# Writing a feed-forward turn's words back over the product tile

## The chip, the cores and the metric

One core of a Trainium2 chip runs the whole kernel. The metric is the device time of one execution in microseconds (us). Every time below is from runs of the kernel before, or from one profiled execution of it. Engines: PE is TensorE (PEld its weight loads), DVE is VectorE, ACT is ScalarE, POOL is GpSimd, SP issues most of the DMAs.

## The reference

A two-layer encoder over 256 tokens of width 2048. A layer is a token mixer with a memory attention, and then a dense SwiGLU feed-forward block, which is the part that matters here:

```python
D_FF = ((8 * D_MODEL // 3 + 255) // 256) * 256   # 5632
def swiglu(h, w_gate_up, w_down):
    gate, up = jnp.split(h @ w_gate_up, 2, axis=-1)
    return (jax.nn.silu(gate) * up) @ w_down
...
x = x + jnp.concatenate([tok_out, mem_out], axis=-1) @ w_out[l]
x = x + swiglu(rms_norm(x, g_ffn[l]), w_gate_up[l], w_down[l])
```

All of it is float32.

## The kernel before

**Products in three parts.** A float32 operand is split into a high part (a cast to fp32r on ACT) and a low part (the operand less the high part, on DVE). A product is three matmuls: high by high (L199), low of the activations by high of the weights (L200), high of the activations by low of the weights (L201). Weights come by DMA into `raw` tiles (4 of them), and `halves` (L263) makes `whi` on ACT (L269) and `wlo` on DVE (L270), in **three** tiles of each name. Activations are split by `split` (L189: high part L193, low part L194) into tiles with the tag `a`.

**The feed-forward block.** The 5632 hidden columns are 11 blocks of 512 (`f`), worked in three chunks of 4, 4 and 3 blocks (L778). For each block a `Pair` (L325) computes gate and up over all 2048 input features; a step `i` takes 256 of them. Then ACT applies Silu into a product tile `sg` (L804), DVE multiplies by the up part in place (L805), and the product is turned, so that hidden columns lie on partitions, and split (L782 to L794). `sg` has two tiles, one for each half `t` of the tokens. When the blocks of a chunk are through, two down `Pair`s multiply the chunk's turned products by the rows of `w_down`, and add into the residual `X`, columns 0 to 1023 in the first pair and 1024 to 2047 in the second.

**Slow and fast steps.** A slow step (`eight`) is 24 matmuls from one weight tile: for t = 0 those into the banks 2 and 3, and then for t = 1 those into 4 and 8. A fast step (`seven`) uses seven products instead of eight (21 matmuls); it needs sums of the weights (`T`, made on DVE at L362 to L365, with a cast and a low part of its own) and sums of the activations (`activation_sums`, two `a` tiles). In a down pair of the first two chunks the fast steps are the first and the third of eight. Four banks go to the tag `acc` and four to `m`; at the end of a pair DVE adds the four `acc` banks to `X` (L428).

**The turn.** `turned` (L207) turns a tile without PE: it takes two `a` tiles, copies the tile's 16-bit halves as two planes into the first (L212), starts a transposing DMA into the second (L213), and some ticks later copies the halves back together into the first (`finish`, L216). That first tile, now the turned words, is what `split_a` reads, once or twice on ACT and once on DVE.

**The `a` tiles of the block.** The pool has 26. At the end of one of the first two chunks are alive: 6 (sums of the input for three fast steps, used by all gate/up pairs), 4 (sums for the two fast down steps, used by both down pairs), and 16 (high and low parts of four blocks and two halves). The planes' tile of the last turn is alive besides until its split has read it.

**What sets the order.** The program's author defers pieces of work by a count of ticks (`later`, `tick`). After that a scheduler puts each engine's instructions into an order of its own, and gives an instruction a tile when one comes free. At run time each engine works through its instructions strictly in that order, and waits at each for what it needs.

Of the kernel before, what the change touches and what calls it, by code (L numbers as in the profile page):

```python
# [12 lines left out]
U16 = mybir.dt.uint16  # L13
# [41 lines left out]
def encoder(ctx: ExitStack, tc: tile.TileContext, x, mem, g_mix, g_ffn, w_in_a, g_v_a, w_spatial, b_spatial,  # L55
            w_in_b, g_q_b, g_k_b, g_mem, w_mem_kv, g_mq, g_mk, w_out, w_gate_up, w_down, rope_c, rope_s, out):
    nc = tc.nc
# [14 lines left out]
    def nm(s):  # L72
        uid[0] += 1
        return f"{s}_{uid[0]}"

    def big(dt=F32, shape=None):
        return room["p"].tile(shape or [P, NB], dt, tag="a", name=nm("a"))
# [19 lines left out]
    def later(delay, fn):  # L97
        queue.append((clock[0] + delay, len(queue), fn))
# [39 lines left out]
    def gslice(kind, l):  # L138
        return gcol[kind][:, 16 * l:16 * l + 16]
# [49 lines left out]
    def split(src, shape):  # L189

        hi = big(F32R, shape)
        lo = big(F32R, shape)
        nc.scalar.copy(hi, src)  # L193
        nc.vector.tensor_tensor(lo, src, hi.bitcast(F32), ALU.subtract)  # L194
        return hi, lo
# [8 lines left out]
        for c in range(4):  # L204
            nc.tensor.transpose(dst[:, c * P:(c + 1) * P], src[:, c * P:(c + 1) * P], ident)  # L205

    def turned(src, ticks, then):  # L207


        a, b = big(F32, [P, 4, P]), big(F32, [P, 4, P])  # L210
        planes, back = [i.bitcast(U16).rearrange("p c n -> p (c n)") for i in (a, b)]
        nc.scalar.copy(planes.rearrange("p (h n) -> p h n", h=2), src.bitcast(U16).rearrange("p (n h) -> p h n", h=2))  # L212
        nc.scalar.dma_start_transpose(back.rearrange("p (c n) -> p c n", n=P), planes)  # L213

        def finish():
            nc.scalar.copy(planes.rearrange("p (n h) -> p n h", h=2), back.rearrange("p (h n) -> p n h", h=2))  # L216
            then(a)

        later(ticks, finish)

# [94 lines left out]
    def activation_sums(a0, a1):  # L315

        q = big(F32, [P, 4, P])
        nc.vector.tensor_tensor(q[:, 0], a1[:, 0], a1[:, 1], ALU.subtract)
        nc.vector.tensor_tensor(q[:, 2], a1[:, 0], a0[:, 0], ALU.subtract)
        nc.vector.tensor_tensor(q[:, 1], a0[:, 0], q[:, 0], ALU.subtract)  # L320
        nc.vector.tensor_tensor(q[:, 3], a0[:, 1], q[:, 1], ALU.subtract)
        hi, lo = split(q, [P, 4, P])
        return [(hi[:, i, :], lo[:, i, :]) for i in range(4)]
# [277 lines left out]
    def add_residual(acc, j, norm, g, parts, dma):  # L601

        def turn(t):
            if dma:
                turned(X[t][j], 2, lambda a: gained(a.rearrange("p c n -> p (c n)"), t, j, g, parts, kept))
            else:
                norm_piece(X[t][j], t, j, g, parts, kept)
            norm.add(X[t][j], t, j)
            if j == 3 and t == NT - 1:
                norm.finish()  # L610

        for t in range(NT):
            if acc:
                nc.vector.tensor_tensor(X[t][j], acc[t], X[t][j], ALU.add)
            later(1 + t, lambda t=t: turn(t))

    def residual_turns(j, norm, g, parts):
        add_residual(None, j, norm, g, parts, j < 2)
# [4 lines left out]
    for l in range(DEPTH):  # L623
# [105 lines left out]
        else:  # L729
# [12 lines left out]
            for c in range(3):  # L742
                acc = linear(hT, w, c * NB)
                attend(head_norm(acc, norm.r, ghead["q"], True), (5, 6, 10, 13), lambda: own["k"], lambda: own["v"],
                       lambda h, c=c: (4 * c + h) // 3, 4 * c, cat)
# [32 lines left out]
        for chunk in (range(0, 4), range(4, 8), range(8, 11)):  # L778
            aT, aS, half = Parts(), {}, {}
            quick = [2 * f + 1 for f in chunk[:2 if chunk[-1] < 10 else l]]  # L780

            def turn_a(a, t, f, aT=aT, aS=aS, half=half, quick=quick):  # L782
                turned(a, 2, lambda whole: split_a(whole, t, f, aT, aS, half, quick))

            def split_a(whole, t, f, aT, aS, half, quick):
                i = 2 * f + 1
                if i in quick:
                    half[i, t] = big(F32, [P, 2, P])
                    nc.scalar.copy(half[i, t], whole[:, 2:4])
                    if t == NT - 1:  # L790
                        aS[i] = activation_sums(half[i, 0], half[i, 1])
                hi, lo = split(whole, [P, 4, P])
                for i in range(4):
                    aT.put(4 * f + i, t, hi[:, i, :], lo[:, i, :])  # L794

            pairs = {}
            for f in chunk:
                order, some = ((3, 4, 5, 0, 6, 1, 7, 2), 2) if f == 0 else ((0, 3, 1, 4, 2, 5, 6, 7), 3)
                pairs[f] = Pair(hF, sums, w_gate_up[l], f * NB, DFF + f * NB, order, fast[:some])
            for f, g in pairs.items():  # L800
                g.run(pairs.get(f + 1))
                for t in range(NT):
                    a = kp.tile([P, NB], F32, tag="sg", name=nm("sg"), bufs=2)
                    nc.scalar.activation(a, g.out[t][0], AF.Silu, scale=norm.r[t])  # L804
                    nc.vector.scalar_tensor_tensor(a, g.out[t][1], norm.r[t], a, ALU.mult, ALU.mult)  # L805
                    later(3 + t if f == chunk[-1] else 12 + t, lambda a=a, t=t, f=f: turn_a(a, t, f))
            last = chunk[-1] == 10
            every = [2 * f + c for f in chunk for c in range(2)]
            slow = [i for i in every if i not in quick]
            pairs = []  # L810
            for jj in range(2):
                order = list(slow)
                for n, i in enumerate(quick):
                    order.insert(2 * n + (2 if last else 0), i)
                into = [[X[t][2 * jj + n] for n in range(2)] for t in range(NT)]
                pairs.append(Pair(aT, aS, w_down[l], 2 * jj * NB, (2 * jj + 1) * NB, order, quick, into))
            for jj, g in enumerate(pairs):
                g.run(None if jj else pairs[1])
                for j in (2 * jj, 2 * jj + 1):
                    if last and l < DEPTH - 1:  # L820
                        residual_turns(j, next_norm, gslice("mix", l + 1), hT)
                    elif last:
                        for t in range(NT):
                            parts = 2 if j == 3 and t == NT - 1 else 1
                            for i in range(parts):
                                cs = slice(i * NB // parts, (i + 1) * NB // parts)
                                eng = nc.scalar if i else nc.sync
                                eng.dma_start(out[0, t * P:(t + 1) * P, j * NB + cs.start:j * NB + cs.stop],
                                              X[t][j][:, cs])
# [37 lines left out]
```

## Time and profile before

| | us |
|---|---|
| median of three runs | 2030.12 |
| lowest and highest of them | 2028.54, 2031.21 |
| the profiled execution | 2030.63 |
| its span, first to last instruction | 2028.8 |
| its mean granted clock of TensorE | 0.998 |

How the views below are read. A row of the timeline is the start in us from the span's start, the duration in us, engine, line, operation, the tile written `<-` the tiles read, and in brackets the idle time of the engine before it with what ended it. A row of a list of waits is who waited for whom, the total in us, the number of waits, and the longest. A row of windows is the stretch, its length, then for PE, PEld, DVE, ACT and POOL the busy time with the number of instructions, then the granted clock of TensorE (1.00 is full speed), the DMA share, and GB/s. Tile names stand without their numbers. The recorded durations of consecutive instructions of one engine overlap a little, so the pace is read from starts.

### The profile page before, as it was taken

How to read it: one execution, taken by the hardware profiler on the slowest of the kernel's cores; microseconds unless marked ns; L12 is line 12 of the kernel's file. 1: busy time of each engine (PE TensorE's matmuls, PEld its weight loads, DVE VectorE, ACT ScalarE, POOL GpSimd, SP SyncE). 2: the span in 40 equal slices, each digit the busy share in tenths (PEclk: the TensorE clock that was granted, in tenths of full speed). 3: DMA queues.
4: the chain of work that ended last, by engine and by line, in shares of the span. 5: the costliest groups of instructions: out<-in, count | busy, mean ns of one | idle time of the engine just before them, and what ended most of it. 6: DMA issues, size and time to landing. Idle time of an engine off the chain costs nothing.

```text
span 2028.8 us, 24312 instructions
## 1 busy us (share of the span) xinstructions
PE 2006.1 (99%) x9058; PEld 1656.6 (82%) x9058; DVE 1603.5 (79%) x1862; ACT 1213.8 (60%) x1509; POOL 50.5 (2%) x80
## 2 busy tenths in 40 slices
PE   8999999999999999999999999999999999999999
PEld 7888888888788887888888888888887888878887
DVE  5576558998889988798666886599987899878977
ACT  7765476666445664456756765756654467634662
POOL 2010000000000000000010100000000000000000
PEclk9999999999999999999999999999999999999999
DMA  9754575666656666577766444756765566755564
GB/s 331 246 183 150 184 218 170 233 198 209 212 184 234 191 214 206 188 231 220 227 203 207 157 144 145 218 187 206 239 218 187 186 203 219 226 188 202 193 212 145
DMA packets 265791, 411.79 MB, mean 203 GB/s; under 512 B 74428, under 2 KB 74792, under 8 KB 265672
## 3 DMA queue, kind: packets, MB, share of 16 engines
q1 hardware_dynamic: 198800, 385.79, 56.3%
q10 hardware_dynamic: 64824, 18.02, 4.8%
q0 software_dynamic: 2048, 6.42, 1.0%
q8 instruction: 71, 1.16, 0.2%
q14 instruction: 48, 0.39, 0.1%
HBM read 390.26 MB, written 4.19 MB: 194 GB/s over the span
## 4 chain that ended last, share of the span: by engine, by line
PE 92%; DVE 3%; DMA 3%; ACT 1%; issue 1%; SPq 0%; DVEq 0%; ACTq 0%
PE acc L201 26%; PE acc L200 26%; PE acc L199 26%; PE m L201 4%; PE m L199 4%; PE m L200 4%; DMA a<-a 2%; DVE wlo L270 2%; ACT whi L269 1%; PE m L205 1%; PE m L515 0%; DMA x<-in_x 0%; PE m L661 0%; DVE T L365 0%; DMA raw<-in_w_in_a 0%
## 5 line engine op out<-in xcount | busy, mean ns | idle before, releaser
L270 DVE TENSOR_TENSOR wlo<-raw,whi 128x2048 fp32r<-128x2048 f32 (+2 forms) x465 | 839.0, 1826 | 242.8 <-ACT whi L269 235.8
L269 ACT CAST whi<-raw 128x2048 fp32r<-128x2048 f32 (+2 forms) x465 | 702.1, 1537 | 459.7 <-PE acc L200 376.5
L199 PE MATMUL acc<-whi,h 128*128 128x512 f32 x1440 | 562.6, 391 | 0.4 <-ACT whi L269 0.4
L200 PE MATMUL acc<-whi,h 128*128 128x512 f32 x1440 | 561.9, 390 | 0.0
L201 PE MATMUL acc<-wlo,h 128*128 128x512 f32 x1440 | 518.2, 391 | 0.8 <-DVE wlo L270 0.8
L199 PE MATMUL acc<-whi,a 128*128 128x512 f32 x1062 | 413.8, 392 | 2.5 <-DVE x L428 1.4
L200 PE MATMUL acc<-whi,a 128*128 128x512 f32 x1062 | 415.6, 391 | 0.0
L201 PE MATMUL acc<-wlo,a 128*128 128x512 f32 x1062 | 400.6, 391 | 0.8 <-DVE wlo L270 0.8
L201 PEld LDWEIGHTS acc<-wlo,h 128*128 128x128 f32 x1440 | 270.6, 188 | 56.9 <-DVE wlo L270 1.4
L199 PEld LDWEIGHTS acc<-whi,h 128*128 128x128 f32 x1440 | 270.6, 188 | 55.5 <-ACT whi L269 0.8
L200 PEld LDWEIGHTS acc<-whi,h 128*128 128x128 f32 x1440 | 270.6, 188 | 55.4
L199 PEld LDWEIGHTS acc<-whi,a 128*128 128x128 f32 x1062 | 199.7, 188 | 46.5 <-DVE x L428 3.0
L201 PEld LDWEIGHTS acc<-wlo,a 128*128 128x128 f32 x1062 | 200.2, 188 | 43.9 <-DVE wlo L270 2.7
L200 PEld LDWEIGHTS acc<-whi,a 128*128 128x128 f32 x1062 | 200.3, 189 | 41.3 <-DVE a L194 0.6
L269 ACT CAST whi<-T 128x1536 fp32r<-128x1536 f32 x82 | 121.4, 1481 | 132.9 <-PE acc L200 99.1
L270 DVE TENSOR_TENSOR wlo<-T,whi 128x1536 fp32r<-128x1536 f32 x82 | 143.9, 1755 | 20.7 <-ACT whi L269 20.7
L199 PE MATMUL m<-whi,a 128*128 128x512 f32 x264 | 103.5, 392 | 5.7 <-ACT whi L269 5.7
L200 PE MATMUL m<-whi,a 128*128 128x512 f32 x264 | 102.8, 390 | 0.0
L216 ACT COPY a<-a 128x1024 uint16<-128x1024 uint16 x60 | 70.2, 1170 | 37.3 <-DMA a<-a 37.1
L201 PE MATMUL m<-wlo,a 128*128 128x512 f32 x264 | 88.7, 395 | 2.4 <-DVE wlo L270 2.4
L362 DVE TENSOR_TENSOR raw<-raw 128x512 f32<-128x512 f32 x82 | 56.5, 688 | 22.8 <-DMA raw<-in_w_gate_up 22.8
L199 PEld LDWEIGHTS m<-whi,a 128*128 128x128 f32 x264 | 49.6, 188 | 18.4 <-ACT whi L269 8.3
(131 smaller groups left out, 1520.0 us busy)
## 6 DMA issues: line engine op xcount, KB each, us to landing
raw<-in_w_gate_up SPq DMA_DIRECT2D x352, 512.0 KB, 4.4
raw<-in_w_down SPq DMA_DIRECT2D x176, 512.0 KB, 5.1
raw<-in_w_out SPq DMA_DIRECT2D x32, 1024.0 KB, 5.2
raw<-in_w_in_a SPq DMA_DIRECT2D x24, 1024.0 KB, 5.1
raw<-in_w_in_b SPq DMA_DIRECT2D x24, 1024.0 KB, 5.0
raw<-in_w_mem_kv SPq DMA_DIRECT2D x16, 1024.0 KB, 5.0
raw<-in_w_in_a SPq DMA_DIRECT2D x7, 512.0 KB, 6.1
x<-in_x SPq DMA_DIRECT2D x8, 256.0 KB, 5.7
```

The lines of the kernel that those rows point to most:

```text
L199: nc.tensor.matmul(out, lhsT=a[0], rhs=b[0], start=start, stop=False)
L200: nc.tensor.matmul(out, lhsT=a[1], rhs=b[0], start=False, stop=False)
L201: nc.tensor.matmul(out, lhsT=a[0], rhs=b[1], start=False, stop=stop)
L205: nc.tensor.transpose(dst[:, c * P:(c + 1) * P], src[:, c * P:(c + 1) * P], ident)
L216: nc.scalar.copy(planes.rearrange("p (n h) -> p n h", h=2), back.rearrange("p (h n) -> p n h", h=2))
L269: nc.scalar.copy(hi[:, cut], raw[:, cut])
L270: nc.vector.tensor_tensor(lo[:, cut], raw[:, cut], hi[:, cut].bitcast(F32), ALU.subtract)
L362: nc.vector.tensor_tensor(raw[:, 0], raw[:, 0], raw[:, 1], ALU.add)
```

## The change

`turned` gets a switch `over`, which only the feed-forward turn sets. With it the second step writes the words back over the tile that they came from, the `sg` tile, and not over the planes' `a` tile; `split_a` then reads the `sg` tile. The turns of the residual are as before.

```diff
-    def turned(src, ticks, then):
+    def turned(src, ticks, then, over=False):
...
         def finish():
-            nc.scalar.copy(planes.rearrange("p (n h) -> p n h", h=2), back.rearrange("p (h n) -> p n h", h=2))
-            then(a)
+            words = src.rearrange("p (c n) -> p c n", c=4) if over else a
+            halves = (src.bitcast(U16) if over else planes).rearrange("p (n h) -> p n h", h=2)
+            nc.scalar.copy(halves, back.rearrange("p (h n) -> p n h", h=2))
+            then(words)
...
             def turn_a(a, t, f, aT=aT, aS=aS, half=half, quick=quick):
-                turned(a, 2, lambda whole: split_a(whole, t, f, aT, aS, half, quick))
+                turned(a, 2, lambda whole: split_a(whole, t, f, aT, aS, half, quick), True)
```

Behind L216 the lines of the changed kernel have numbers that are 2 higher (L270 becomes L272, L428 becomes L430). Every engine has as many instructions as before. On ACT, POOL and SP their order is the same too; on DVE and PE it differs in four stretches, the down pairs of the first and second chunk of each layer. The first of the four:

On PE, at the handover of the first down pair (banks `acc_691`, `acc_692`, `acc_693`, `acc_700`) to the second (`m_737` to `m_740`, `acc_741` and on), in the kernel before. The first number of a name is the tile's. Weights 726 and 730 are the first pair's last two steps, 733 and 735 the second pair's first, fast step (735 is from its T); `a_710` and `a_711` are the high and low part of the chunk's last block for t = 1, `a_561` and `a_562` sums for the fast step:

```order
L201 MATMUL acc_742_4415<-wlo_734_4388,a_561_3418 128x512
L199 MATMUL m_739_4403<-whi_735_4391,a_561_3418 128x512
L200 MATMUL m_739_4403<-whi_735_4391,a_562_3419 128x512
L199 MATMUL m_740_4407<-whi_735_4391,a_561_3418 128x512
L200 MATMUL m_740_4407<-whi_735_4391,a_562_3419 128x512
L201 MATMUL m_739_4403<-wlo_736_4392,a_561_3418 128x512
L201 MATMUL m_740_4407<-wlo_736_4392,a_561_3418 128x512
L200 MATMUL acc_693_4116<-whi_726_4316,a_711_4204 128x512
L201 MATMUL acc_693_4116<-wlo_727_4317,a_710_4203 128x512
L199 MATMUL acc_693_4116<-whi_726_4316,a_710_4203 128x512
L200 MATMUL acc_693_4116<-whi_726_4316,a_711_4204 128x512
L201 MATMUL acc_693_4116<-wlo_727_4317,a_710_4203 128x512
```

The same place in the changed kernel:

```order
L200 MATMUL acc_700_4154<-whi_730_4352,a_711_4204 128x512
L201 MATMUL acc_700_4154<-wlo_731_4353,a_710_4203 128x512
L199 MATMUL m_737_4395<-whi_733_4387,a_553_3380 128x512
L200 MATMUL m_737_4395<-whi_733_4387,a_554_3381 128x512
L201 MATMUL m_737_4395<-wlo_734_4388,a_553_3380 128x512
L199 MATMUL m_738_4399<-whi_733_4387,a_561_3418 128x512
L200 MATMUL m_738_4399<-whi_733_4387,a_562_3419 128x512
L201 MATMUL m_738_4399<-wlo_734_4388,a_561_3418 128x512
L199 MATMUL m_739_4403<-whi_735_4391,a_561_3418 128x512
L200 MATMUL m_739_4403<-whi_735_4391,a_562_3419 128x512
```

Before, 22 matmuls of the first pair (from `acc_693<-whi_726,a_711` on) stand behind the first 18 of the second pair. In the changed kernel all matmuls of the first pair stand ahead of the second pair's first.

On DVE, at the same handover, in the kernel before, with the engines or DMA queues that each instruction waits for:

```order
L428 TENSOR_TENSOR x_0_0_89<-acc_691_4108,x_0_0_89 128x512 [waits PE_49]
L428 TENSOR_TENSOR x_0_1_90<-acc_692_4112,x_0_1_90 128x512 [waits PE_49]
L270 TENSOR_TENSOR wlo_736_4392<-T_729_4347,whi_735_4391 128x1536 [waits PE_49,Activation_49]
L194 TENSOR_TENSOR a_711_4204<-a_701_4161,a_710_4203 128x512 [waits PE_49]
L428 TENSOR_TENSOR x_1_0_93<-acc_693_4116,x_1_0_93 128x512 [waits PE_49]
L270 TENSOR_TENSOR wlo_747_4432<-raw_732_4384,whi_746_4431 128x2048 [waits DMAHW6_49,DMAHW5_49,Activation_49]
L428 TENSOR_TENSOR x_1_1_94<-acc_700_4154,x_1_1_94 128x512 [waits PE_49]
```

In the changed kernel the low part `a_711` stands 20 instructions further up, ahead of the first pair's last two weights:

```order
L415 TENSOR_TENSOR e_713_4208<-m_689_4100,e_712_4207 128x512 [waits Activation_49]
L422 TENSOR_TENSOR x_0_0_89<-x_0_0_89,e_712_4207 128x512
L194 TENSOR_TENSOR a_711_4204<-sg_679_4070,a_710_4203 128x512 [waits DMAHW6_49,Activation_49]
L416 TENSOR_TENSOR e_714_4209<-m_688_4096,e_713_4208 128x512 [waits DVE_49]
L272 TENSOR_TENSOR wlo_727_4317<-raw_722_4282,whi_726_4316 128x2048 [waits DMAHW0_49,DMAHW7_49,PE_49,Activation_49]
```

And at the handover itself stand there in the changed kernel:

```order
L430 TENSOR_TENSOR x_0_0_89<-acc_691_4108,x_0_0_89 128x512 [waits PE_49]
L272 TENSOR_TENSOR wlo_736_4392<-T_729_4347,whi_735_4391 128x1536 [waits Activation_49]
L430 TENSOR_TENSOR x_0_1_90<-acc_692_4112,x_0_1_90 128x512 [waits PE_49]
L430 TENSOR_TENSOR x_1_0_93<-acc_693_4116,x_1_0_93 128x512 [waits PE_49]
L430 TENSOR_TENSOR x_1_1_94<-acc_700_4154,x_1_1_94 128x512 [waits PE_49]
L272 TENSOR_TENSOR wlo_747_4432<-raw_732_4384,whi_746_4431 128x2048 [waits DMAHW6_49,DMAHW5_49,Activation_49]
```

So `a_711` reads the `sg` tile, waits for a DMA queue and ACT and no longer for PE, and stands ahead of the weights 727. `wlo_736` stands ahead of the second of the four additions instead of behind it, and waits for ACT alone; and the subtraction for the weights 746 stands behind all four L430. The low part for t = 0 moves up by one row, ahead of a subtraction of weights.

## The prediction

> **What bounds the kernel now.** I read the page first: engines, then the chain.
>
> ```profile
> span 2028.8 us, 24312 instructions
> PE 2006.1 (99%) x9058; PEld 1656.6 (82%) x9058; DVE 1603.5 (79%) x1862; ACT 1213.8 (60%) x1509; POOL 50.5 (2%) x80
> ```
>
> TensorE (PE) is busy for 2006.1 of 2028.8 us. No other engine can set the end by its amount of work; a change can only win where PE stands still or runs slowly. So the second view is PE's list of waits (total, times, longest):
>
> ```profile
> PE m L199 <- ACT whi L269: 5.7, 6, 1.3
> PE m L135 <- DMA gst_mix<-in_g_mix: 4.7, 1, 4.7
> PE m L201 <- DVE wlo L270: 2.4, 4, 0.6
> ...
> PE acc L199 <- DVE x L428: 1.4, 3, 0.6
> ```
>
> 4.7 us is the start of the program. The rest is small, but the three lines with L199/L201 into `m` and L428 belong together: asked for by stretch, they fall at four places, one in each of the first two chunks of the feed-forward block of both layers, where the first down pair hands over to the second. The first of the four, on PE's timeline (start, duration, idle before in brackets):
>
> ```profile
> 526.06 0.39 PE L199 MATMUL m<-whi,a 128*128 128x512 f32 x1
> 527.77 0.50 PE L199 MATMUL acc<-whi,a 128*128 128x512 f32 x1 [0.19 <-DVE x L428]
> 529.04 0.39 PE L201 MATMUL acc<-wlo,a 128*128 128x512 f32 x1
> 530.77 0.50 PE L199 MATMUL m<-whi,a 128*128 128x512 f32 x1 [1.33 <-ACT whi L269]
> 532.56 0.73 PE L201 MATMUL m<-wlo,a 128*128 128x512 f32 x2 [0.60 <-DVE wlo L270]
> 536.02 0.39 PE L201 MATMUL acc<-wlo,a 128*128 128x512 f32 x1
> ```
>
> What released it, on ScalarE (ACT) and VectorE (DVE):
>
> ```profile
> 529.24 1.47 ACT L269 CAST whi<-T 128x1536 fp32r<-128x1536 f32 x1 [7.14 <-PE acc L200]
> 530.75 1.76 DVE L270 TENSOR_TENSOR wlo<-T,whi 128x1536 fp32r<-128x1536 f32 x1 [2.43 <-ACT whi L269]
> 532.42 0.69 DVE L194 TENSOR_TENSOR a<-a,a 128x512 fp32r<-128x512 f32 x1
> ```
>
> ACT sat idle for 7.14 us, then cast T, and what released it was PE. That is a circle: PE waits for ACT, which waited for PE. The order in the section on the change says why. The low part of the chunk's last product (L194 at 532.42, tile a_711) finds no free `a` slot until PE has read the sums of the second pair's first fast step. So 22 matmuls of the first pair that need a_711, or follow one that does, stand behind 18 of the second pair. They keep the weights 726 and 730, two of the three `whi` slots; the second pair's weights 733 hold the third, and the cast of T (735) must wait until PE is done with 733 at 529.04. Then cast (1.47 us), subtraction (1.76 us) and PE run one after the other.
>
> **What one place costs.** PE's undisturbed pace, 27 matmuls from first to last row:
>
> ```profile
> 560.05 0.39 PE L199 MATMUL acc<-whi,a 128*128 128x512 f32 x1
> 565.94 0.39 PE L201 MATMUL acc<-wlo,a 128*128 128x512 f32 x1
> ```
>
> 5.89 us / 26 = 0.2265 us a matmul. At each place I take 31 matmuls, from the second pair's first (526.06) to the thirteenth of the postponed ones (536.02); 30 steps at that pace are 6.80 us. The other three places:
>
> ```profile
> 780.39 0.39 PE L199 MATMUL m<-whi,a 128*128 128x512 f32 x1
> 790.77 0.39 PE L201 MATMUL acc<-wlo,a 128*128 128x512 f32 x1
> 1528.31 0.39 PE L199 MATMUL m<-whi,a 128*128 128x512 f32 x1
> 1534.57 1.22 PE L201 MATMUL m<-wlo,a 128*128 128x512 f32 x2 [0.60 <-DVE wlo L270]
> 1539.43 0.39 PE L201 MATMUL acc<-wlo,a 128*128 128x512 f32 x1
> 1783.70 0.39 PE L199 MATMUL m<-whi,a 128*128 128x512 f32 x1
> 1795.43 0.39 PE L201 MATMUL acc<-wlo,a 128*128 128x512 f32 x1
> ```
>
> They take 9.96, 10.38, 11.12 and 11.73 us; less 6.80 each, the losses are 3.16, 3.58, 4.32 and 4.93 us, together 16.0 us. That is more than the idle in brackets (2.1 us at the first place), since the matmuls after a gap start slower, and in layer 1 the clock falls too. The windows (length, busy of PE, PEld, DVE, ACT, POOL, then the granted clock):
>
> ```profile
> 780.00:790.00 10.00, 7.44 (x30) 5.01 (x29) 5.45 (x7) 1.47 (x1) 0.00 (x0) 1.00 0.37 124
> 1530.00:1540.00 10.00, 8.07 (x27) 5.87 (x27) 2.70 (x3) 2.54 (x2) 0.00 (x0) 0.83 0.23 82
> 1790.00:1800.00 10.00, 9.41 (x35) 7.66 (x36) 4.58 (x6) 4.22 (x3) 0.00 (x0) 0.83 0.00 1
> ```
>
> These are the only two 10-us windows before 2020 us whose granted clock is under 1.00, and both begin in the stall. From the wait for `wlo` to the last row, 14 steps, the third place takes 4.86 us and the first 3.46: the clock is worth 1.4 us a time, 2.8 of the 16.0.
>
> On this the Trainium skill speaks against me. Its page "TensorE: Matmul & The Clock Gate" (section "Why this matters for your kernels") holds that the clock falls back after idle gaps above about 3 us. No gap here is over 1.33 us, so by that rule the dips would not be the stall's doing and would stay, and the sum would be 13.2 us and not 16.0. The trace does not bear the rule out, as the clock fell to 0.83 of a window with a longest gap of 1.33 us.
>
> The dips lie in the two stalls of layer 1, not in those of layer 0, and nowhere else before 2020 us. I count them to the stall and keep the other reading as a rival.
>
> **The change part by part.** *The copy.* The second copy keeps its shape and count, 44 of the 60 at this line change only the tile they write, and no instruction is added or removed on any engine: 0 us.
>
> ```profile
> L216 ACT COPY a<-a 128x1024 uint16<-128x1024 uint16 x60 | 70.2, 1170 | 37.3 <-DMA a<-a 37.1
> 503.37 1.17 ACT L216 COPY a<-a 128x1024 uint16<-128x1024 uint16 x1 [0.23 <-DMA a<-a]
> 508.54 0.63 ACT L193 CAST a<-a 128x512 fp32r<-128x512 f32 x1
> 511.41 0.68 DVE L420 TENSOR_TENSOR x<-x,e 128x512 f32<-128x512 f32 x1
> ```
>
> *The freed slot.* The planes' tile is now dead once the transposing DMA has read it, by 503.37. a_711 takes a slot that this DMA frees, not one that PE frees, and its high part is cast by 509.17; it moves up to behind the L420 at 511.41 and runs near 512.0, 20 us earlier. PE's order becomes the natural one: all of the first pair, then the second. With weights 726 read to the end 24 matmuls after their first (5.4 us), T can be cast long before PE asks for it. All three waits of a place go: −16.0 us over four places.
>
> *What it delays.* The early L194 pushes DVE by its 0.69 us. The next weights' low part, in before:
>
> ```profile
> 512.61 2.29 DVE L270 TENSOR_TENSOR wlo<-raw,whi 128x2048 fp32r<-128x2048 f32 x1
> 520.62 0.39 PE L201 MATMUL acc<-wlo,a 128*128 128x512 f32 x1
> ```
>
> It would end near 515.6 and PE first reads it at 520.62: 5 us of cover, 0 us. The two after it have 10 and 22 more matmuls ahead of them on PE than before.
>
> *What is late next.* At the handover the second pair's step after T (weights 746). In before:
>
> ```profile
> 535.54 1.91 ACT L269 CAST whi<-raw 128x2048 fp32r<-128x2048 f32 x1 [4.83 <-PE acc L200]
> 537.13 0.69 DVE L428 TENSOR_TENSOR x<-acc,x 128x512 f32<-128x512 f32 x1 [4.02 <-PE acc L201]
> 537.74 2.28 DVE L270 TENSOR_TENSOR wlo<-raw,whi 128x2048 fp32r<-128x2048 f32 x1
> ```
>
> In the change its slot comes free when the first pair ends. PE then has the 21 matmuls of the fast step and two that need the high part alone: 23 × 0.2265 = 5.2 us. Cast and subtraction need 1.91 + 2.28 = 4.2 us. The last L428, which now waits for PE ahead of this subtraction on DVE, takes 0.69 us under the cast. About 1 us is left: 0 us, with 0 to 2 us a place as bounds if a handoff is slower than these rows show. It cannot be under 0, as PE has then nothing left to gain there.
>
> *The added wait.* The product tile (two buffers) is now held until its split has read it, so the next Silu waits for L194 and not for the first copy. Behind the Silu on ACT stand the casts that PE needs. The closest case:
>
> ```profile
> 395.33 0.68 DVE L194 TENSOR_TENSOR a<-a,a 128x512 fp32r<-128x512 f32 x1
> 400.69 0.69 DVE L428 TENSOR_TENSOR e<-acc,e 128x512 f32<-128x512 f32 x1
> 401.42 0.72 ACT L804 ACTIVATE sg<-e,s 128x512 f32<-128x512 f32 x1 [0.78 <-DVE e L428]
> ```
>
> The Silu waits in any case for the L428 of its own block, and in the changed order every L194 stands ahead of that L428 on the same engine. It can never be the later of the two: 0 us.
>
> **Sum.** The profiled execution took 2030.63 us, 1.8 more than its span and 0.5 above the median of the runs shown (2030.12). 2030.63 − 16.0 = **2014.6 us**.
>
> **The rivals.** *The clock dips stay* (they have another cause than the stall): only 16.0 − 2.8 = 13.2 us are won, 2017.4 us. Against it stands that both lie in a stall; for it, that two stalls of the same length in layer 0 have none.
>
> *A smaller wait takes the place*: the 1 us of slack at weights 746 is gone and PE waits up to 2 us at each place: up to 2022.6 us. For it speaks the tight sum, against it that PE shows no wait between the later steps of the same pairs, which also follow each other through three `whi` slots.
>
> *Slower*: the same handover, but wholly uncovered. If the fast step's matmuls do not run under the cast and subtraction, because DVE is held at the four L428 until the first pair ends and then has a backlog, PE waits for all of 4.2 us, and each wait draws a clock dip of 1.4 us: 4 × 5.6 = 22.4, 2037 us. It turns the sign from 4.0 us a place. Against it stands that the two subtractions of the fast step are ahead of, or between, those L428 in the new order.
>
> *The change doesn't do what it says*: the last low part still finds its slot late, or the 16 us come back as waits elsewhere because PE was never short of work there: 2030 us. Against it stands that PE has no wait at all for some 200 us behind each place.
>
> **How the numbers follow.** 2014.6 gets 0.62, the dips staying 0.15, the smaller wait 0.10, no change 0.08, slower 0.05. The runs shown lie 2.7 us apart, so the forecast's own low end is 2012; the range reaches to 2021 for the dips and most of the smaller waits. About 0.2%, 4 us, is what a measurement of this kernel can tell from no change: faster means under 2026. The first three cases are faster, 0.87.
>
> **What would show it.** In the changed profile PE's list has lost the 1.3 and 0.6 us waits of `m` at the four places (totals 5.7 and 2.4 fall to under 1) and the L428 line; the last L194 of a chunk stands some 15 us ahead of the second pair; 31 matmuls at each handover take about 6.8 us; the granted clock is 1.00 there. I am wrong if a wait for `wlo` or `whi` opens at the second pair's second step, if a Silu waits for L194, or if DVE, no longer interrupted, falls behind and PE waits later in the pair.

## The result, and the profile after

| | before | after |
|---|---|---|
| median, us | 2030.66 | 2015.71 |
| lowest and highest | 2028.54 to 2031.36 | 2014.45 to 2016.73 |
| runs | 4 | 4 |
| the profiled execution | 2030.63 | 2014.45 |
| its span | 2028.8 | 2012.7 |

The ratio is 0.9928, with an interval of 0.9911 to 0.9945: faster by 15.0 us. The forecast was 2014.6 us, in a range of 2012 to 2021; the median lies 1.1 us above it. Medians below leave out two disturbed executions, of 3384 and 2510 us.

The page of the changed kernel, its span and its engines (busy time, share of the span, instructions):

```profile
span 2012.7 us, 24336 instructions
PE 2000.3 (99%) x9058; PEld 1655.5 (82%) x9058; DVE 1605.4 (80%) x1862; ACT 1216.0 (60%) x1509; POOL 50.6 (3%) x80
```

PE still sets the end, with the same 9058 matmuls, and the counts of work on the other engines are those of before too. The 24 instructions more in the first row are semaphore waits, 18 on ACT and 6 on DVE. The span fell by 16.1 us. Of these, 10.3 are idle time of PE (2028.8 − 2006.1 = 22.7 before, 2012.7 − 2000.3 = 12.4 after), and 5.8 are busy time (2006.1 − 2000.3): as many matmuls have shorter records, since none of them stands behind a stall at a handover, as the ones of 0.50 and 0.73 us did, or at a lower clock. So this kernel lost more to its stalls than its idle time showed.

PE's list of waits in the changed kernel (who waited for whom, total in us, times, longest), whole:

```profile
PE m L135 <- DMA gst_mix<-in_g_mix: 4.6, 1, 4.6
PE acc L199 <- ACT whi L271: 1.2, 4, 0.5
PE acc L201 <- DVE wlo L272: 0.8, 4, 0.2
PE m L205 <- DMA x<-in_x: 0.6, 2, 0.3
PE m L199 <- ACT whi L271: 0.4, 2, 0.2
```

The wait of `m` for `whi` went from 5.7 to 0.4, that of `m` for `wlo` from 2.4 to nothing, and the line of `acc` for L428 (now L430) is gone. In the down pairs the two `acc` lines that are left lie at the start of the first pair (0.3 and 0.2 us the first time), not at its end.

The first handover on PE's timeline, from the second pair's first matmul to its thirty-first:

```profile
531.66 0.39 PE L199 MATMUL m<-whi,a 128*128 128x512 f32 x1
...
533.02 0.39 PE L199 MATMUL m<-whi,a 128*128 128x512 f32 x1
...
534.61 0.62 PE L201 MATMUL m<-wlo,a 128*128 128x512 f32 x2
...
536.42 0.39 PE L199 MATMUL acc<-whi,a 128*128 128x512 f32 x1
...
538.23 0.39 PE L201 MATMUL acc<-wlo,a 128*128 128x512 f32 x1
538.46 0.39 PE L199 MATMUL acc<-whi,a 128*128 128x512 f32 x1
```

538.46 − 531.66 = 6.80 us for 30 steps: this stretch now runs at the undisturbed pace, where before the second pair's first and the 30 behind it took 9.96. The other three handovers also take 6.80 us now (from 783.11, 1526.40 and 1777.46). By the order of the changed kernel the row at 533.02 is the first to read T's high part, that at 534.61 its low part; 536.42 and 538.23 are the same for the weights 746.

DVE around the same place:

```profile
501.96 0.69 DVE L194 TENSOR_TENSOR a<-sg,a 128x512 fp32r<-128x512 f32 x1 [3.32 <-ACT a L193]
...
512.98 0.68 DVE L194 TENSOR_TENSOR a<-sg,a 128x512 fp32r<-128x512 f32 x1
513.58 0.69 DVE L416 TENSOR_TENSOR e<-m,e 128x512 f32<-128x512 f32 x1
514.18 2.28 DVE L272 TENSOR_TENSOR wlo<-raw,whi 128x2048 fp32r<-128x2048 f32 x1
...
529.32 1.75 DVE L272 TENSOR_TENSOR wlo<-T,whi 128x1536 fp32r<-128x1536 f32 x1
530.99 1.88 DVE L430 TENSOR_TENSOR x<-acc,x 128x512 f32<-128x512 f32 x3
533.63 2.29 DVE L272 TENSOR_TENSOR wlo<-raw,whi 128x2048 fp32r<-128x2048 f32 x1 [0.76 <-ACT whi L271]
```

The chunk's last low part runs at 512.98 instead of 532.42, 18.7 us ahead of the second pair. T's low part is ready at 529.32 + 1.75 = 531.07, 3.5 us before its reader at 534.61; before, PE waited for it.

The cast of T, on ACT:

```profile
526.24 1.49 ACT L271 CAST whi<-T 128x1536 fp32r<-128x1536 f32 x1 [3.52 <-PE acc L200]
531.68 1.92 ACT L271 CAST whi<-raw 128x2048 fp32r<-128x2048 f32 x1 [3.95 <-PE acc L200]
```

Read the bracket with care. ACT still idles for PE ahead of this cast, but it is done at 527.73, and PE asks for it only at 533.02. What made the same kind of row a loss in the kernel before was that PE at that time was waiting for this very cast.

The windows at the four handovers (columns as before the change; the granted clock is the figure behind POOL):

```profile
530.00:540.00 10.00, 10.00 (x46) 8.28 (x45) 7.50 (x7) 5.22 (x3) 0.00 (x0) 1.00 0.43 145
780.00:790.00 10.00, 10.00 (x46) 8.29 (x45) 7.42 (x8) 4.76 (x3) 0.00 (x0) 1.00 0.42 129
1530.00:1540.00 10.00, 10.00 (x46) 8.26 (x44) 6.10 (x4) 6.60 (x4) 0.00 (x0) 1.00 0.69 211
1790.00:1800.00 10.00, 10.00 (x46) 8.29 (x45) 9.96 (x9) 5.81 (x4) 0.00 (x0) 1.00 0.70 239
```

PE is busy throughout, and the clock is 1.00 in all four, also in the two of layer 1 where it had been 0.83. No other 10-us window from 10 to 2010 us is under 1.00.

### The profile page after: what moved, and what is told of

Same layout as the page of the kernel before. It is cut to its first block, busy times and chain, and to the rows that moved or that the text cites. A ratio compares the mean times of both kernels' runs of the same rounds, so it can differ in the third digit from the quotient of the medians.

```text
span 2012.7 us, 24336 instructions
## 1 busy us (share of the span) xinstructions
PE 2000.3 (99%) x9058; PEld 1655.5 (82%) x9058; DVE 1605.4 (80%) x1862; ACT 1216.0 (60%) x1509; POOL 50.6 (3%) x80
## 4 chain that ended last, share of the span: by engine, by line
PE 96%; DMA 2%; ACT 1%; DVE 1%; issue 0%; SPq 0%; ACTq 0%
PE acc L201 28%; PE acc L199 27%; PE acc L200 27%; PE m L201 4%; PE m L199 4%; PE m L200 4%; PE m L205 1%; ACT whi L271 1%; DVE wlo L272 1%; DMA a<-a 1%; DMA raw<-in_w_down 0%; PE m L517 0%; DMA x<-in_x 0%; PE m L663 0%; DMA raw<-in_w_in_a 0%; ACT sg L218 0%
## 5 line engine op out<-in xcount | busy, mean ns | idle before, releaser
L272 DVE TENSOR_TENSOR wlo<-raw,whi 128x2048 fp32r<-128x2048 f32 (+2 forms) x465 | 838.9, 1826 | 228.1 <-ACT whi L271 220.3
L272 DVE TENSOR_TENSOR wlo<-T,whi 128x1536 fp32r<-128x1536 f32 x82 | 143.9, 1755 | 14.1 <-ACT whi L271 14.0
L218 ACT COPY sg<-a 128x1024 uint16<-128x1024 uint16 x44 | 51.6, 1173 | 26.5 <-DMA a<-a 26.3
L430 DVE TENSOR_TENSOR e<-acc,e 128x512 f32<-128x512 f32 x88 | 57.4, 689 | 2.3 <-PE acc L201 1.7
## 6 DMA issues: line engine op xcount, KB each, us to landing
raw<-in_w_gate_up SPq DMA_DIRECT2D x352, 512.0 KB, 4.4
raw<-in_w_down SPq DMA_DIRECT2D x176, 512.0 KB, 5.0
raw<-in_w_in_a SPq DMA_DIRECT2D x7, 512.0 KB, 6.3
```

Source lines behind the costliest of these rows:

```text
L218: nc.scalar.copy(halves, back.rearrange("p (h n) -> p n h", h=2))
L272: nc.vector.tensor_tensor(lo[:, cut], raw[:, cut], hi[:, cut].bitcast(F32), ALU.subtract)
L430: nc.vector.tensor_tensor(o[t][n], self.bank[name], o[t][n], op)
```

## The experiments

The theory of the prediction: one `a` slot was missing at the end of the first two chunks, for the low part of the last block's t = 1, and nothing else of the change counts. Its rivals: the whole change does it (44 turns fewer that hold an `a` tile for their words), or the clock dips have a cause of their own. Runs of the kernel before on the same chip had a median of 2030.48 us beside four of the experiments (t = 1 alone, all turns but that one, 25 tiles, one fast step) and 2031.03 beside the other four. "Before" in the ratios is these runs.

**One turn of eight.** Only the last block of a chunk, and of it only t = 1, writes back over `sg`; the other turns do as before.

```diff
-            def turn_a(a, t, f, ..., quick=quick):
-                turned(a, 2, lambda whole: split_a(...), True)
+            def turn_a(a, t, f, ..., quick=quick, chunk_last=chunk[-1]):
+                turned(a, 2, lambda whole: split_a(...), f == chunk_last and t == NT - 1)
```

> The write-back over the product tile is switched on for 4 of the 44 feed-forward turns alone: the last block of a chunk, t = 1, in the first two chunks of both layers (and the 2 of the last chunks, which have free slots anyway). Slot theory (the whole gain is the one `a` slot that the chunk's last low part lacked): PE's order is that of the changed kernel, no wait of 1.3 us at m, no clock dip, about 2015.7 us, ratio to the kernel before 0.993. Rival (the gain is spread over the 44 write-backs, by slots that come free earlier everywhere): 4 to 6 of 44 turns give a tenth of it, about 2029 us.

Measured: 2017.76 us, ratio 0.9943 (0.9927 to 0.9960). 6 of the 44 turns (4 of them at one of the handovers) bring 5.7 of the 6.9 thousandths that the whole change brings when it is run again below. The waits of `m` are gone as in the changed kernel, and PE's order is the same as there. But one line is longer, on PE's list:

```profile
PE acc L201 <- DVE wlo L272: 4.8, 4, 1.4
```

It had been 0.8 with the whole change (1.9 in a second profile, of which 1.0 is one wait at another place). On DVE at the start of the first down pair:

```profile
503.31 0.69 DVE L194 TENSOR_TENSOR a<-a,a 128x512 fp32r<-128x512 f32 x1 [5.81 <-DMA a<-a]
503.92 6.83 DVE L272 TENSOR_TENSOR wlo<-raw,whi 128x2048 fp32r<-128x2048 f32 x3
```

The low part of the other half, t = 0, now waits for its slot, which the transposing DMA of t = 1 has to free. It runs at 503.31 where the changed kernel has it at 501.96, and DVE stands for 5.81 us with the first weights of the down pair queued behind it. Their cast is done at 503.00, and their subtraction starts at 503.92. So the change does a second thing: it lets t = 0 have a slot of its own. 4.8 − 0.8 = 4.0 us of idle, and 2017.76 − 2015.66 (the change, run again below) = 2.1 us of the medians. The two ratios' intervals overlap, so the claim that this costs time rests on PE's list, and on the run with both halves below.

**All turns but that one.** The complement:

```diff
-                turned(a, 2, lambda whole: split_a(...), True)
+                turned(a, 2, lambda whole: split_a(...), f != chunk_last or t != NT - 1)
```

> The complement: the write-back is on for every feed-forward turn except the last block's t = 1 of a chunk. Slot theory: the four stalls are back as before (waits of about 1.3 and 0.6 us at m, 31 matmuls in 10 to 12 us instead of 6.8), about 2030.5 us, ratio 1.000. Rival (spread over the write-backs): nearly all of the gain stays, about 2017 us. For the clock: if the stall draws the dips, every 10-us window with a granted clock under 1.00 lies in one of the four stalls, with 0 to 4 of them; if they have another cause, some lie elsewhere.

Measured: 2031.28 us, ratio 1.0006 (0.9997 to 1.0016). Nothing is won, and PE's order is that of the kernel before. PE's list:

```profile
PE m L199 <- ACT whi L271: 5.7, 6, 1.3
...
PE m L201 <- DVE wlo L272: 2.4, 4, 0.6
```

These are the totals of before, 5.7 and 2.4, to the tenth. With the run above this puts the handovers' gain on the last turn of a chunk.

**The change with one slot less.** If it is a slot that counts, taking one from the pool must take the gain back.

```diff
-FFN_TILES = 26
+FFN_TILES = 25
```

> The changed kernel with 25 `a` tiles in the feed-forward pool instead of 26. Slot theory: 26 are alive at the end of a chunk, so the last low part again waits for PE to read the fast step's sums; PE's order is that of the kernel before and the four stalls are back, 2029 to 2032 us. Rival (what counts is that the words come to lie in the product tile, not the number of slots): the gain stays, 2016 to 2018 us. For the clock the same as in the run before it: dips only inside stalls, or also elsewhere.

Measured: 2032.73 us, ratio 1.0017 (1.0005 to 1.0029). The whole change is in, yet the waits of `m` are back at 5.7 and 2.4, and t = 0 is late as in the first experiment:

```profile
PE acc L201 <- DVE wlo L272: 5.7, 4, 2.0
PE m L199 <- ACT whi L271: 5.7, 6, 1.3
...
PE m L201 <- DVE wlo L272: 2.4, 4, 0.6
```

PE's order is again that of the kernel before. At the first handover the last low part reads the `sg` tile, so the words are where the change puts them, and still it runs only after T's subtraction, as in the kernel before (532.42 there):

```profile
532.88 0.68 DVE L194 TENSOR_TENSOR a<-sg,a 128x512 fp32r<-128x512 f32 x1
```

**The last block, both halves.** The smallest part of the change that should give all of it:

```diff
-                turned(a, 2, lambda whole: split_a(...), True)
+                turned(a, 2, lambda whole: split_a(...), f == chunk_last)
```

> The write-back over the product tile for the last block of each chunk, both t. In the run with t = 1 alone, 2018.3 us, the low part of t = 0 still waited for a slot that a DMA freed (DVE idle 5.81 us until 503.31) and then pushed the first weights of the down pair back by 0.7 us, so that PE waited 1.06 us there and not 0.2, at four places. Theory: t = 0 is the rest of the gain; DVE runs it before the first weights, the wait of acc for wlo falls from 4.8 us to about 0.8 us, and the time is that of the changed kernel, 2015.7 us (2014.5 to 2017). Rival (the 2.6 us come from the other 36 turns, or from the chip): 2018 us as with t = 1 alone.

The unchanged kernel after ran beside it, for the clock and for the comparison:

> The changed kernel once more, on the chip of this call's other runs: 2015.7 us, no 10-us window with a granted clock under 1.00. If the clock dips have a cause of their own, one or two windows under 1.00 should show up here, as in the kernel before.

Measured: 2014.49 us, ratio 0.9923 (0.9909 to 0.9938); the change itself 2015.66, ratio 0.9931 (0.9914 to 0.9947). 12 of the 44 turns give all the gain. The difference of 1.2 us between the two is within their scatter (2013.97 to 2015.40, and 2015.10 to 2016.97, four runs each, overlap). The low part of t = 0 is on time again:

```profile
501.94 0.69 DVE L194 TENSOR_TENSOR a<-sg,a 128x512 fp32r<-128x512 f32 x1 [3.68 <-ACT a L193]
```

**Two slots made free in another way.** The kernel before, with one fast step in a down pair of the first two chunks instead of two. Sums for one step fewer are alive, so there is room without the change; PE has 24 matmuls instead of 21 in the step that turns slow.

```diff
-            quick = [2 * f + 1 for f in chunk[:2 if chunk[-1] < 10 else l]]
+            quick = [2 * f + 1 for f in chunk[:1 if chunk[-1] < 10 else l]]
```

> The kernel before (write-back over the planes' tile) with one fast step instead of two in the down pairs of the first two chunks. It frees two `a` slots by another way, and costs 8 times 3 more matmuls, 24 x 0.2265 = 5.4 us. Slot theory: the stalls of 16 us go, 2030.6 - 16.0 + 5.4 = 2020 us, ratio 0.995. Rival (the slot is not what holds the last low part; the product tile is): 2030.6 + 5.4 = 2036 us, ratio 1.003.

Measured: 2027.75 us, ratio 0.9991 (0.9982 to 1.0001), where the theory gave 2020, nearly 8 us less: a miss. What it said of the handovers holds in the profiled execution: PE has no wait at all in the stretches of the four down pairs (480 to 540 us is the first), and no window from 10 to 2010 us is under a clock of 1.00. But two lines of PE's list have grown:

```profile
PE acc L199 <- ACT whi L269: 5.7, 4, 2.1
...
PE acc L201 <- DVE wlo L270: 3.5, 4, 1.1
```

They lie at four other places, in gate/up pairs, one wait of each kind at each. ACT at the first of them:

```profile
458.55 1.17 ACT L216 COPY a<-a 128x1024 uint16<-128x1024 uint16 x1 [3.02 <-DMA a<-a]
...
459.93 1.90 ACT L269 CAST whi<-raw 128x2048 fp32r<-128x2048 f32 x1 [0.20 <-DMA raw<-in_w_gate_up]
```

and PE behind it:

```profile
461.88 0.50 PE L199 MATMUL acc<-whi,h 128*128 128x512 f32 x1 [1.23 <-ACT whi L269]
```

In the kernel before, ACT has the same work in another order there:

```profile
457.21 3.73 ACT L269 CAST whi<-raw 128x2048 fp32r<-128x2048 f32 x2 [0.38 <-PE acc L200]
460.84 1.17 ACT L216 COPY a<-a 128x1024 uint16<-128x1024 uint16 x1
```

With other tile lives the scheduler has put the turn's second copy ahead of a weight cast. The copy waits for its transposing DMA, the cast behind it waits with it, and PE waits for the cast. (The cast's bracket names the DMA of its weights, but in the trace no DMA of weights lands between 457.6 and the cast's start, so the copy, done at 459.72, held it.) The second wait at each place has a cause of its own. DVE stands at the first addition for a later T, which needs a DMA of down weights, and the subtraction that PE needs is behind it:

```profile
472.99 0.69 DVE L362 TENSOR_TENSOR raw<-raw 128x512 f32<-128x512 f32 x1 [3.77 <-DMA raw<-in_w_down]
```

In the kernel before, that subtraction stands ahead of this L362. The two lines make 9.2 us where the kernel before has 1.4 + 1.6 = 3.0. The span adds up: 2028.8 before, less 16.0 for the handovers, plus 5.4 for 24 more matmuls (3 in each of 8 down pairs, at 0.2265 us), plus the 6.2 us of new waits, is 2024.4, and it is 2024.5. This takes the new waits at their idle and the handovers by PE's starts; by starts too, the new waits cost 11.6 us and the old ones that are gone 5.5, a difference of 6.1. So the miss is new waits at other places, and the handovers' 16 us stand.

**More fast steps where a slot is over.** The third chunk of layer 0 has no fast step, the third of layer 1 one. With the change's free slots it could have two in both: 3 fast steps more, in two pairs each, 18 matmuls fewer or 4.1 us. In this kernel part of the fast steps' products is added to `X` only after `X` has been read for the next layer or the output, so it doesn't compute the block, and only its time is of use.

```diff
-            quick = [2 * f + 1 for f in chunk[:2 if chunk[-1] < 10 else l]]
+            quick = [2 * f + 1 for f in chunk[:2]]
```

> The changed kernel with two fast steps in the down pairs of the last chunk too (none in layer 0 and one in layer 1 until now). That chunk has three blocks, so 12 + 6 + 4 = 22 of 26 slots are alive at its end. It saves 3 fast steps x 2 pairs x 3 matmuls = 18 matmuls, 4.1 us: 2011.6 us if DVE and ACT keep up. Rival: DVE has the weights' sums of six more steps to make (each about 2.4 us) where the next layer's first turns already ask for it, and PE waits for them: 2016 us or more.

Measured: 2023.47 us, ratio 0.9966 (0.9956 to 0.9976): 7.8 us slower than the change. PE's list:

```profile
PE acc L199 <- ACT whi L271: 6.4, 7, 2.5
...
PE m L205 <- DMA x<-in_x: 2.4, 3, 1.2
PE acc L199 <- DVE x L430: 2.0, 2, 1.1
PE m L199 <- ACT whi L271: 1.7, 4, 0.7
```

In the changed kernel these four make 1.2 + 0.6 + 0 + 0.4 = 2.2 us, here 12.5: 10.3 us more, against 4.1 of matmuls saved. The profiled execution is the slowest of the eight (2026.4 us). Its two longest waits, 1.67 us until 968.71 and 2.51 us until 1015.19, have the pattern seen with one fast step: on ACT a turn's copy (L218), which waited 2.87 and 1.95 us for its transposing DMA, stands ahead of the cast that PE needs.

The smaller form, one fast step in the third chunk of both layers:

```diff
-            quick = [2 * f + 1 for f in chunk[:2 if chunk[-1] < 10 else l]]
+            quick = [2 * f + 1 for f in chunk[:2 if chunk[-1] < 10 else 1]]
```

> The changed kernel with one fast step in the last chunk of layer 0 too: saves 2 x 3 = 6 matmuls, 1.4 us: 2014.3 us if nothing else moves. Rival: the same wait for DVE at the end of layer 0, 2016 us or more.

Measured: 2017.01 us, ratio 0.9936 (0.9921 to 0.9950). The median is 1.3 us above that of the change, but the runs overlap (2016.24 to 2017.97, and 2015.10 to 2016.97). PE's list:

```profile
PE acc L199 <- ACT whi L271: 2.5, 3, 1.8
PE m L205 <- DMA x<-in_x: 2.0, 3, 0.9
PE acc L201 <- DVE wlo L272: 1.4, 6, 0.3
PE m L199 <- ACT whi L271: 0.4, 2, 0.2
```

6.3 us against 3.0 in the changed kernel's list, for 1.4 of matmuls saved (6 fewer). In both profiles a fast step at the end of a layer saves less than the waits that come with it; the cause of each of the other waits is open. Neither beats the change.

Not tried, as the kernel's pools leave no room for it in SBUF: the kernel before with 27 `a` tiles, or with a fourth `whi` tile. The slot theory therefore rests on taking a slot away and on freeing some, not on adding one.

## Why the prediction was right

**The bound and the four places: shown.** The waits that it put together went as a group (5.7 to 0.4, 2.4 to nothing, 1.4 to nothing), and PE's other waits hardly changed.

**The cause, one slot for the chunk's last low part: shown, from three sides.** With that turn alone the handovers are whole, without it they are as before, and with one slot less in the pool the full change brings nothing. That freeing slots in another way also clears the handovers, and that with 25 tiles the last low part is late although it reads the `sg` tile, makes it a matter of slots and not of the copy's target.

**The size, 16.0 us: right.** The profiled executions differ by 2030.63 − 2014.45 = 16.2, the medians by 15.0. All four handovers now run at the undisturbed pace, so the whole term was won; the forecast priced it from one execution, with its two dips, while the mean clocks of the kernel before run from 0.997 to 1.000. The step that carried it was to price a place by its lost steps (9.96 − 6.80) and not by its idle: the idle in brackets was 2.1 us at the first place, and the list's three lines together 9.5 us, or 6.5 short of the loss.

**The clock dips, 2.8 of the 16.0: they belong to the stall.** The changed kernel has none from 10 to 2010 us, in either of its two profiles, and the rival in which they stay (2017.4 us) falls. In the three profiles with the stalls (before, all turns but that one, 25 tiles) 7 of 12 handovers dip; in the seven without them none of 28 does. The rule of the Trainium skill that the prediction weighed ("TensorE: Matmul & The Clock Gate", section "Why this matters for your kernels", gaps above about 3 us) does not cover these dips: they went with gaps that were at most 1.34 us long.

**The copy and the added Silu wait, at nothing: no sign against them.** On ACT's list of waits the Silu (now L806) waits for its own block's L430 and never for L194, as forecast, and the copy's group keeps its mean, 1173 ns where it had 1170. A row of ACT's waits, and the group (busy, mean ns, idle before it):

```profile
ACT sg L806 <- DVE e L430: 13.0, 13, 3.0
```

```profile
L218 ACT COPY sg<-a 128x1024 uint16<-128x1024 uint16 x44 | 51.6, 1173 | 26.5 <-DMA a<-a 26.3
```

**What is late next, weights 746: right in sign, off in size.** Their low part is done at 533.63 + 2.29 = 535.92, and PE first reads it at 538.23. The slack is 2.3 us and not about 1. The step counted 23 matmuls between the freed slot and the first use; PE's order puts more matmuls ahead that need the high part alone (the first of these weights runs at 536.42, the first that reads the low part 8 steps later).

**The early low part: 1 us off in place.** It runs at 512.98 and not near 512.0. The weights 727 behind it are done at 516.46, with the same answer of 0 us.

**What it had not seen: the low part of t = 0.** The text on the change noted that it moves up by one row, and the prediction gave it no term. It costs nothing in the full change because its slot, too, is freed early; where it isn't (the first experiment), it costs some 2 us by the medians. The sum was right with this term unnamed, since its part in the change is nothing lost, not something gained.

**The slower rival** needed DVE to be held at the additions (L430) until the first pair ends and then to fall behind. DVE is through the last three of them at 530.99 + 1.88 = 532.87, before ACT has finished the cast for 746 at 531.68 + 1.92 = 533.60. That cast, and not a backlog of DVE, sets the start of the subtraction (the bracket of 0.76 us).

## What to carry to other kernels

Where the engine that bounds the kernel waits for an engine that was itself released by the bounding one, look for a tile that one queue holds too long: the loss may be one missing slot, not a lack of speed. Price such a place by its matmuls' starts against the undisturbed pace, since the idle time leaves out the slow matmuls behind a gap. And when tile lives change, read every engine's order anew: in the run with one fast step, more free slots let the scheduler put a waiting instruction ahead of one that the bound needs.

## What the runs showed of the hardware

The clock falls after short gaps, and not after each. Two windows of the run with all turns but the last, whose PE timeline has the same handovers as the kernel before:

```profile
780.00:790.00 10.00, 7.52 (x25) 5.01 (x24) 5.22 (x7) 1.47 (x1) 0.00 (x0) 0.87 0.35 119
...
1790.00:1800.00 10.00, 9.40 (x35) 7.30 (x34) 4.65 (x5) 3.73 (x2) 0.00 (x0) 0.83 0.00 0
```

In the kernel before the handovers 3 and 4 dipped, here 2 and 4 (the dip of 2 reaches into the next window, with 0.96), and with 25 tiles 1, 3 and 4, each time behind gaps of at most 1.34 us. Two dips lie elsewhere: with 25 tiles around the start of a down pair, in two windows, where the longest gap is 2.0 us, and with two fast steps in the third chunk at the end of layer 0, where the longest is 2.5 us (the wait until 1015.19). The windows with 25 tiles:

```profile
1760.00:1770.00 10.00, 7.91 (x31) 5.87 (x30) 5.63 (x4) 8.72 (x8) 0.00 (x0) 0.94 0.57 147
1770.00:1780.00 10.00, 10.00 (x41) 8.12 (x41) 8.96 (x11) 3.86 (x3) 0.00 (x0) 0.89 0.93 324
```

And with two fast steps in the third chunk:

```profile
1010.00:1020.00 10.00, 7.49 (x26) 5.69 (x25) 6.05 (x11) 9.39 (x19) 0.00 (x0) 0.83 0.59 155
```

So each dip follows a gap of PE of at least 1.3 us. The profiled execution of the kernel with one fast step has gaps of up to 2.1 us and no dip, so a gap's length alone doesn't decide; what does stays open. (Other executions of that kernel have mean clocks down to 0.997.) The clock also goes with the scatter of the times: 23 runs of the kernel before lie between 2027.30 and 2033.05 us, and grouped by mean granted clock they average 2032.3 at 0.997 (4 runs), 2030.4 at 0.998 (10), 2029.4 at 0.999 (7) and 2029.1 at 1.000 (2). It is not all of the scatter, as one run with 25 tiles took 2035.83 us at 1.000.
